# Keeping the weight's split operands for both token halves in the out-product of an MLP

## The chip, the cores and the metric

The kernel is one program on one core of a Trainium2 chip. The metric is the device time of one launch in microseconds (us): the median of several runs, each of them one execution. One more execution is recorded by the hardware profiler, and all rows shown here come from such a record. Engines are called as in the profile: PE is the matmul engine, PEld its weight load, DVE the vector engine, ACT the scalar engine, POOL the GpSimd engine, SP the queue that issues DMAs. Each engine takes its instructions in a fixed order, written when the program is built.

## The reference, cut to what matters

One layer of an encoder: an attention group beside a recurrent group, a cross-attention, then an MLP, for 2048 tokens of width 1024 in float32.

```python
D_MODEL, SEQ, D_FF = 1024, 2048, 4096
...
        hid = jnp.square(jax.nn.relu(rmsnorm(h, norm_mlp_g[l]) @ w_mlp_in[l]))
        h = h + hid @ w_mlp_out[l]
    return rmsnorm(h, norm_final_g).astype(x.dtype)
```

The change is in the second product, `hid @ w_mlp_out`, 4096 to 1024 wide. Everything before it is as it was.

## The kernel before

**Precision.** A float32 operand is split in two: a head h, an ACT copy into the type that PE reads (fp32r), and a remainder l, the operand less its head, by a subtraction on DVE or POOL. A product is then three matmuls, `mm3`: ah·bh, ah·bl, al·bh (lines 119 to 121).

**Fast products.** Both MLP products cut their operands in 2 x 2 blocks and use seven products of sums of blocks instead of eight (Winograd's form of Strassen's scheme). The in-product (`InPair`, 32 pairs) writes its result to DRAM as `hid_d`. The out-product runs in 16 passes: part q (0 to 7) takes 512 of the 4096 rows, and B (0 or 1) is the half of the tokens; pass n is q = n // 2, B = n % 2. In this document odd passes are those with B = 1. Operand A comes from the weight `w_m2` (four blocks of 128 x 1024, two of row halves by two of column halves) and depends on q alone; operand B comes from `hid_d` and depends on q and on the half. Pass 15 is plain: four operands, no sums.

**A part's work.** `Part.load` issues four DMAs of 512 KB (line 1269). `Part.sum_steps` makes the sums (an addition in line 1282, all others in `minus`, line 1257): of A all four on POOL, 1024 wide, of B two on DVE and two on POOL. `Part.split(n)` splits operand n (ACT in line 1304, remainder in line 1305): of A in two halves of 512, the remainders of operands 2 and 5 on DVE and of the other five on POOL; of B in one piece of 1024, remainder on DVE. Loads and sums of A are made once for each q, when B is 0. Its splits are made in every pass, for both halves of the tokens anew: seven operands, 14 ACT copies, 10 POOL and 4 DVE subtractions.

**Places.** On-chip memory is full, so tiles take over the places of tiles that are done. A `Ring` hands out a list of named places in turn. `A_RINGS` has five places for raw blocks, three for sums, eight for heads, eight for remainders; `B_RINGS` has five, three, four, four. A new tile waits for the last reader of the one whose place it takes, whichever engine that is.

**A pass.** Seven slots s, one product each: four 128-wide pieces d, by two, by `mm3`, so 24 matmuls of 128 x 512. A product adds into four PSUM banks (`SLOTS`, `BANKS`: names m, a, b in the profile), and after each piece DVE adds the bank into an accumulator in on-chip memory (line 1459, the evictions; accumulators are named t3l to t6h and wr). The next product that uses the same bank waits for that eviction. Slot 2 issues the next pass's loads, slot 4 its sums, slots 0 to 4 the splits of operands 2 to 6, slots 5 and 6 the next pass's operands 0 and 1. A planner then orders each engine's instructions by that priority and by when it expects operands and places to be there, so splits run ahead of products. The last pass is split in token ranges of 512, 256 and 256 and is followed by a final normalisation (`RowSum`, lines 137 to 164, and `finish`, lines 1419 to 1423).

Of the kernel before, what the change touches and what calls it, by code (L numbers as in the profile page):

```python
# [10 lines left out]
F32, F32R, F16, BF, I32 = DT.float32, DT.float32r, DT.float16, DT.bfloat16, DT.int32  # L11
AF = mybir.ActivationFunctionType
ALU = mybir.AluOpType
# [26 lines left out]
def hybrid_block(ctx: ExitStack, tc: tile.TileContext, prm, x, xT, mem, memT, pos, masks, w_in, gate_w,  # L40
                 w_out, w_cq, w_ck, w_cv, w_co, w_m1, w_m2, out):
    nc = tc.nc
    act, dve, pool, pe = nc.scalar, nc.vector, nc.gpsimd, nc.tensor
    dma = nc.sync.dma_start
    dma_r = nc.gpsimd.dma_start
    P = 128

    def f32(a):
        return a.bitcast(F32)
# [22 lines left out]
    hid_d = [[dt_(f"hid_d{i}_{p}", [2, 2, P, 512]) for p in range(16)] for i in range(2)]  # L72
# [50 lines left out]
    class RowSum:  # L123


        def __init__(self, pl, bufs=1, n=512, late=False, eng=pool, rings={}):
            self.pl, self.i, self.n, self.late, self.eng, self.rings = pl, 0, n, late, eng, rings
            self.ss = self.tile("ss", bufs)

        def tile(self, name, bufs):  # L130
            if name in self.rings:
                return self.rings[name]()[:, 0:self.n]
            return self.pl.tile([P, 512], F32, tag=name, name=name, bufs=bufs)[:, 0:self.n]
# [72 lines left out]
    with ExitStack() as s12:  # L206
# [400 lines left out]
        with sb("xr") as xr_pool:  # L607
            with sb("p1") as p1:
                W, steps = unit_w(w_in[0], True)
# [27 lines left out]
    with ExitStack() as s3:  # L637
# [321 lines left out]
        with sb("aw") as aw:  # L959
            half_out(aw, W)  # L960
            for k in range(8):
                t = aw.tile([P, 512], F32, tag="raw4", name="raw4", bufs=2)
# [6 lines left out]
    with ExitStack() as s6:  # L969
# [9 lines left out]
        for kk in range(4):  # L979
            for n in range(2):  # L980
                t = wp.tile([P, 512], F32, tag="ht", name="raw4", bufs=3)
# [149 lines left out]
        class InPair:  # L1131
# [5 lines left out]
            def load(self):  # L1137
                self.r = []
                for f in range(2):
                    t = wr_.tile([P, 8 * P])  # L1140
                    dma(t.rearrange("p (k n) -> p k n", n=P), w_m1[2 * self.p + f])
                    self.r.append(t)
# [9 lines left out]
            def split(self, n):  # L1152
                h, l = wh_.tile([P, 512], F32R), wl_.tile([P, 512], F32R)
                act.activation(h, self.a[n], AF.Copy)  # L1154
                last[n % 2] = (pool if n % 2 else dve).tensor_tensor(l, self.a[n], f32(h), op=ALU.subtract).ins  # L1155
                self.w[n] = h, l
# [99 lines left out]
    def minus(eng, o, x, y):  # L1256
        eng.tensor_tensor(o, x, y, op=ALU.subtract)  # L1257

    class Part:


        def __init__(self, rings, blocks, plain, eng, sum_eng):
            self.rings, self.blocks, self.plain, self.eng, self.sum_eng = rings, blocks, plain, eng, sum_eng
            self.s, self.b = {}, {}

        def load(self):
            for k, src in self.blocks:
                t = self.b[k] = self.rings["r"].tile([P, 2, 512])
                dma(t, src)

        def sums(self):
            for _ in self.sum_steps():
                pass

        def sum_steps(self):
            b, e = self.b, self.sum_eng
            if self.plain:
                self.ops = [b[0, 0], b[0, 1], b[1, 0], b[1, 1]]
                return
            x1, x2, x4 = (self.rings["s"].tile([P, 2, 512]) for _ in range(3))  # L1280
            if self.rings is A_RINGS:
                e[0].tensor_tensor(x1, b[1, 0], b[1, 1], op=ALU.add)
                yield
                minus(e[1], x2, x1, b[0, 0])
                yield
                minus(e[2], b[1, 0], b[0, 0], b[1, 0])
                yield
                minus(e[3], x4, b[0, 1], x2)
                self.ops = [b[0, 0], x2, x1, x4, b[1, 0], b[1, 1], b[0, 1]]
            else:  # L1290
                minus(e[0], x1, b[0, 1], b[0, 0])
                minus(e[1], x2, b[1, 1], x1)
                minus(e[2], b[0, 1], b[1, 1], b[0, 1])
                minus(e[3], x4, b[1, 0], x2)
                self.ops = [b[0, 0], x2, x1, b[1, 1], b[0, 1], x4, b[1, 0]]

        def split(self, n):
            t, w = self.ops[n], self.rings["w"]
            h, l = [], []
            for k in range(0, 2, w):  # L1300
                h.append(self.rings["h"].tile([P, 512 * w], F32R))
                l.append(self.rings["l"].tile([P, 512 * w], F32R))
                tk = t[:, k:k + w, :].rearrange("p k n -> p (k n)")
                act.activation(h[-1], tk, AF.Copy)  # L1304
                self.eng[n].tensor_tensor(l[-1], tk, f32(h[-1]), op=ALU.subtract)  # L1305
            cut = lambda x_: [x_[k // w][:, 512 * (k % w):512 * (k % w) + 512] for k in range(2)]
            self.s[n] = cut(h), cut(l)

    A_ENG = [pool, pool, dve, pool, pool, dve, pool]
    B_ENG = [dve] * 7  # L1310
    tt = [(jp, f"t{n}{z}{h}") for n in range(7) for z in "hl" for h in range(2)]
    rw = [(ip, f"raw{k}{h}") for k in ("00", "01", "11", "10", "t") for h in range(2)]
    c2 = [(jp, f"c{i}") for i in (2, 3, 4, 5, 6, 0, 1)]
    w2 = [(ip, f"w{k}{i}") for k in "hl" for i in range(3)]
    s2 = [(ip, f"ws{i}") for i in range(3)]
    A_RINGS = {"r": Ring(*rw[:5]), "s": Ring(*rw[5:8]), "h": Ring(*s2[:2], *c2[:2], *c2[3:7]),
               "l": Ring(s2[2], c2[2], *w2), "w": 1}
    B_RINGS = {"r": Ring(*rw[8:], *tt[:3]), "s": Ring(*tt[3:6]), "h": Ring(*tt[6:14:2]), "l": Ring(*tt[7:14:2]), "w": 2}
    acc_at = Ring(*tt[14:], (ip, "wr0"), (ip, "wr1"))

    def a_part(q, plain):

        blocks = []
        for i, k in ((0, 0), (1, 0), (1, 1), (0, 1)):
            r = 512 * q + 256 * k
            blocks.append(((i, k), w_m2[r:r + 256, 512 * i:512 * i + 512].rearrange("(t p) d -> p t d", p=P)))
        return Part(A_RINGS, blocks, plain, A_ENG, [pool] * 4)

    def b_part(q, B, plain):

        blocks = [((k, th), hid_d[B][2 * q + k][:, th].rearrange("f p n -> p f n"))
                  for k, th in ((0, 0), (0, 1), (1, 1), (1, 0))]
        return Part(B_RINGS, blocks, plain, B_ENG, [dve, dve, pool, pool])

    passes = []
    for q in range(8):
        a = a_part(q, False)
        for B in range(2):
            passes.append((q, B, a, b_part(q, B, q == 7 and B == 1)))

    last_a = a_part(7, True)
    passes[-1] = (7, 1, last_a, passes[-1][3])
    rings = {"ss": lambda: A_RINGS["s"].tile([P, 2, 512])[:, 0, :], "sq": lambda: B_RINGS["s"].tile([P, 2, 512])[:, 0, :],
             "dg": lambda: B_RINGS["s"].tile([P, 2, 512])[:, 0, :]}

    def begin(n, what):

        q, B, a, b = passes[n]
        if what == "load":
            if a.plain:  # L1350
                a.b.update(passes[n - 1][2].b)
                a.blocks = a.blocks[1:2]
            if B == 0 or a.plain:
                a.load()
            b.load()
        elif what == "sums":
            if B == 0 or a.plain:
                a.sums()
            b.sums()
        else:  # L1360
            a.split(what)
            b.split(what)

    T = {}
# [6 lines left out]
    steps = t_raws(1)  # L1371
    nT = {}
    for i, pr in enumerate(ins):
        if i == 16:
            T = nT
        for n in range(7):
            if n == 2 and 0 < i < 31:
                ins[i + 1].load()
            if n == 4 and i < 31:
                ins[i + 1].sums()  # L1380
            if n < 5:
                pr.split(n + 2)
            elif i < 31:
                ins[i + 1].split(n - 5)
            pr.product(n, T[n])
            if 9 <= i < 15:
                ahead(1)
            if i == 0 and n == 2:
                rb2.append(rows())
                before.ss.columns()  # L1390
                before.ss.rows(rb2[3])
            if i == 15 and n > 0:
                t_part(nT, n - 1)
            if i == 16 and n == 0:
                t_part(nT, 6)
            if i == 20 and n == 0:
                first_a.load()
                first_sums = first_a.sum_steps()
            if i in (21, 22, 23, 24, 25) and n == 3:
                with tc.issue_after(last[1]):  # L1400
                    next(first_sums, None)
            if i == 31:
                if n == 1:
                    first_b.load()
                if n == 4:
                    first_a.split(0)
                    first_a.split(1)
                if n == 5:
                    first_b.sums()
                    first_b.split(0)  # L1410
                    first_b.split(1)
# [159 lines left out]
```

## Time and profile before

| what | value |
|---|---|
| median of 3 runs | 2863.25 us (2860.2 to 2868.93) |
| profiled execution, its own time | 2856.53 us |
| its span, first to last instruction | 2854.7 us |
| mean granted clock of PE | 0.947 |
| in-product, splits of its weights to last eviction | 1449 to 2168 us of the span |
| out-product, passes 0 to 14 | 2167 to 2781 us |
| last pass and final normalisation | 2781 to 2855 us |
| ACT copies of A, passes 1 to 13 | 182 x 0.633 us |
| A remainders, passes 1 to 13 | 130 on POOL, 52 on DVE |

A row of a group reads: line, engine, operation, out<-in, shape, number of instructions | busy time, mean ns of one | idle time of the engine before them and what ended it. A row of waits reads: who waited <- for whom: us in total, times, longest. A row of a timeline reads: start, duration, engine, line, operation, tiles; x2 means two merged, and a bracket is idle time before it. Tiles are named by their place, so one name serves many contents: raw is an A block or sum, c, ws, wh and wl hold A heads and remainders, rawt and t0 B blocks and sums, t1 to t3 B's heads and remainders.

### The profile page before, as it was taken

What the parts mean: (1) busy time and instruction counts of PE and PEld (TensorE: products, weight loads), DVE (VectorE), ACT (ScalarE), POOL (GpSimd) and SP (SyncE); (2) the same over time, 40 slices, a digit from 0 to 9 for tenths busy, and PEclk for the clock granted to TensorE, in tenths of its full rate; (3) what the DMA queues carried; (4) which work ended last, traced back from release to release, by engine and by line L of the source; (5) the groups of instructions that cost most, each with busy time, mean ns of one, the idle gap of its engine ahead of it and who ended that gap; (6) DMA issues with size and microseconds to landing.
All of it is one profiled execution on the core that took longest, in us unless ns stands there. A gap on an engine that the chain in (4) does not pass through costs nothing. (4 is left out here: it accounts for less than half of the span.)

```text
span 2854.7 us, 39920 instructions
## 1 busy us (share of the span) xinstructions
PE 2541.4 (89%) x14104; PEld 2139.9 (75%) x14104; DVE 2013.0 (71%) x3257; ACT 1278.4 (45%) x2359; POOL 1351.6 (47%) x916
## 2 busy tenths in 40 slices
PE   8899785884887797999996999899998999999997
PEld 6778674773887786777875888788886777777876
DVE  7547676774888678446578554755548999999997
ACT  6438545452765566435333333433333333333452
POOL 3222121222776573542145555646655767666662
PEclk9999897986998898999998999999999999999998
DMA  6443334337786784653253333343335222222213
GB/s 212 145 129 98 117 108 144 102 106 184 202 234 170 185 209 114 217 168 101 89 173 112 114 111 111 111 144 112 109 109 203 74 82 81 82 67 89 82 45 118
DMA packets 258044, 368.43 MB, mean 129 GB/s; under 512 B 85682, under 2 KB 132018, under 8 KB 254772
## 3 DMA queue, kind: packets, MB, share of 16 engines
q1 hardware_dynamic: 253556, 338.62, 37.6%
q0 software_dynamic: 4288, 27.27, 3.9%
q8 instruction: 111, 1.82, 0.3%
q14 instruction: 89, 0.73, 0.1%
HBM read 251.19 MB, written 114.63 MB: 128 GB/s over the span
## 5 line engine op out<-in xcount | busy, mean ns | idle before, releaser
L1304 ACT ACTIVATE c<-raw 128x512 fp32r<-128x512 f32 x162 | 102.1, 632 | 273.0 <-PE m L120 140.8
L1155 POOL TENSOR_TENSOR wl<-wr,wh 128x512 fp32r<-128x512 f32 x96 | 145.5, 1516 | 145.7 <-ACT wh L1154 145.7
L1154 ACT ACTIVATE wh<-wr 128x512 fp32r<-128x512 f32 x128 | 80.9, 632 | 287.2 <-PE m L120 151.6
L757 ACT ACTIVATE sm<-sm,obp 128x256 f32<-128x256 f32 (+1 forms) x384 | 161.0, 469 | 59.6 <-DVE obp L754 52.8
L1155 DVE TENSOR_TENSOR wl<-ws,wh 128x512 fp32r<-128x512 f32 x96 | 81.0, 843 | 127.0 <-ACT wh L1154 127.0
L754 DVE CUSTOM_DVE_ANT_0 sm<-a,msk 128x256 f32<-128x256 f32 (+1 forms) x384 | 129.7, 372 | 38.7 <-PE a L751 36.5
L226 POOL TENSOR_TENSOR wl<-wraw,wh 128x512 fp32r<-128x512 f32 x48 | 71.3, 1487 | 166.9 <-ACT wh L225 160.2
L1176 DVE TENSOR_TENSOR c<-m,c 128x512 f32<-128x512 f32 x64 | 44.1, 690 | 138.4 <-PE m L121 136.4
L119 PE MATMUL m<-xh,wh 128*128 128x512 f32 x328 | 131.6, 401 | 8.0 <-ACT xh L320 8.0
L766 PE MATMUL b<-prt,sm 128*128 128x128 f32 x640 | 109.3, 286 | 29.2 <-DVE pl L770 13.7
L769 ACT ACTIVATE ph<-b 128x512 f16<-128x512 f32 (+1 forms) x192 | 100.1, 523 | 69.6 <-PE b L766 68.9
L1305 POOL TENSOR_TENSOR wh<-raw,c 128x512 fp32r<-128x512 f32 x58 | 94.7, 1650 | 76.6 <-ACT c L1304 71.5
L120 PE MATMUL m<-xl,wh 128*128 128x512 f32 x328 | 130.1, 397 | 0.0
L770 DVE SCALAR_TENSOR_TENSOR pl<-b,ph 128x512 f16<-128x512 f32 (+1 forms) x192 | 114.7, 598 | 21.4 <-ACT ph L769 19.0
L121 PE MATMUL m<-xh,wl 128*128 128x512 f32 x328 | 129.7, 396 | 0.0
L696 POOL TENSOR_SCALAR kc<-kh 128x1024 fp32r<-128x1024 f32 x32 | 66.0, 2062 | 121.7 <-PE a L751 97.5
L1177 DVE SCALAR_TENSOR_TENSOR c<-c 128x512 f32<-128x512 f32 x96 | 114.1, 1189 | 1.0
L121 PE MATMUL m<-t3h,wl 128*128 128x512 f32 x276 | 108.4, 393 | 2.0 <-POOL wl L1155 2.0
L1154 ACT ACTIVATE wh<-ws 128x512 fp32r<-128x512 f32 x96 | 60.4, 629 | 108.0 <-PE m L120 107.2
L766 PEld LDWEIGHTS b<-prt,sm 128*128 128x128 f32 x640 | 76.6, 146 | 34.8 <-issue 14.9
L1305 POOL TENSOR_TENSOR wl<-raw,c 128x512 fp32r<-128x512 f32 x58 | 93.3, 1625 | 19.8 <-ACT c L1304 19.8
L1033 POOL TENSOR_SCALAR pm<-pm,dn 128x256 f32<-128x256 f32 x64 | 36.6, 590 | 127.6 <-DVE dn L1031 112.4
(573 smaller groups left out, 9787.4 us busy)
## 6 DMA issues: line engine op xcount, KB each, us to landing
wr<-in_w_m SPq DMA_DIRECT2D x64, 512.0 KB
hid_d<-c SPq DMA_DIRECT2D x128, 256.0 KB
wraw<-in_w_in SPq DMA_DIRECT2D x80, 256.0 KB
raw<-in_w_m SPq DMA_DIRECT2D x33, 512.0 KB
rawt<-hid_d SPq DMA_DIRECT2D x26, 512.0 KB
t0h<-hid_d SPq DMA_DIRECT2D x26, 512.0 KB
o_d<-obp SPq DMA_DIRECT2D x16, 528.0 KB
obr<-o_d SPq DMA_DIRECT2D x16, 528.0 KB
```

The lines of the kernel that those rows point to most:

```text
L119: pe.matmul(o, ah, bh, start=start, stop=False, **kw)
L120: pe.matmul(o, ah, bl, start=False, stop=False, **kw)
L121: pe.matmul(o, al, bh, start=False, stop=stop, **kw)
L754: dve.tensor_tensor_reduce(out=sm, in0=sps[:, 256 * z + o0:256 * z + o0 + kw], in1=msk[:, m:m + kw], op0=ALU.add, op1=ALU.min, scale=1.0, ...
L757: exps.append(act.activation(sm, sm, AF.Exp, scale=-1.0, bias=self.obp[:, oc, 65:66]))
L766: pe.transpose(pt[:, c0:c0 + 128], self.sm[:, z, 128 * g:128 * g + 128], idt)
L770: dve.scalar_tensor_tensor(self.pl[:, :w], pt[:, :w], 1024.0, self.ph[:, :w], op0=ALU.mult, op1=ALU.subtract)
L1154: act.activation(h, self.a[n], AF.Copy)
L1155: last[n % 2] = (pool if n % 2 else dve).tensor_tensor(l, self.a[n], f32(h), op=ALU.subtract).ins
L1177: dve.scalar_tensor_tensor(z, z if n < 6 else o, 0.0, z, op0=ALU.max, op1=ALU.mult)
L1304: act.activation(h[-1], tk, AF.Copy)
L1305: self.eng[n].tensor_tensor(l[-1], tk, f32(h[-1]), op=ALU.subtract)
```

## The change

A's split operands are made when B is 0 and kept for B = 1. There is not room for 14 remainders beside 14 heads, raw blocks and sums, so remainders go to nine places shared with the raw blocks and sums: the remainder of an operand takes the place of the operand split before it, or of a free place. The table `free` says which place of part q becomes which of part q + 1. Sixteen places serve as one ring for heads. The fourth sum (x4) is taken out of the sums and made just before operand 1 is split. In the last pass three of the four A operands are the ones kept, and only block (1, 0), which a sum had overwritten, is loaded and split again. The two kinds of part get classes of their own; what `BPart` issues is what `Part` issued for B.

```diff
+    class APart:
+        L_AT = {(0, 0): "a", 2: (0, 0), 1: 2, 4: 1, (1, 0): 4, (1, 1): (1, 0), (0, 1): (1, 1)}
+        def tile(self, k, d=F32):
+            pl, tag = self.at[k]
+            return pl.tile([P, 2, 512], d, tag=tag, name=tag)
...
+        def sum_steps(self):
+            b = self.b
+            x1, x2 = b[1], b[2] = self.tile(1), self.tile(2)
+            pool.tensor_tensor(x1, b[1, 0], b[1, 1], op=ALU.add)
+            yield
+            minus(pool, x2, x1, b[0, 0])
+            yield
+            minus(pool, b[1, 0], b[0, 0], b[1, 0])
+            yield
+            b[4] = self.tile(4)
+            minus(pool, b[4], b[0, 1], x2)
+
+        def split(self, n, key=None):
+            key = A_OPS[n] if key is None else key
+            t = self.b[key]
+            lt = self.tile(self.L_AT[key], F32R)
             h, l = [], []
+            for k in range(2):
+                h.append(h_a.tile([P, 512], F32R))
+                l.append(lt[:, k, :])
+                act.activation(h[-1], t[:, k, :], AF.Copy)
+                A_ENG[n].tensor_tensor(l[-1], t[:, k, :], f32(h[-1]), op=ALU.subtract)
+            self.s[n] = h, l
+    A_OPS = [(0, 0), 2, 1, 4, (1, 0), (1, 1), (0, 1)]
     A_ENG = [pool, pool, dve, pool, pool, dve, pool]
...
-    A_RINGS = {"r": Ring(*rw[:5]), "s": Ring(*rw[5:8]), "h": Ring(*s2[:2], *c2[:2], *c2[3:7]),
-               "l": Ring(s2[2], c2[2], *w2), "w": 1}
+    h_a = Ring(*s2[:2], *c2[:2], *c2[3:7], s2[2], c2[2], *w2)
...
+    order = [(0, 0), (1, 0), (1, 1), (0, 1), 1, 2, 4, "a", "b"]
+    free = ["b", (0, 1), "a", (0, 0), 2, 1, 4, (1, 0), (1, 1)]
+    at = dict(zip(order, [*rw[:8], (ip, "wr2")]))
     for q in range(8):
+        if q > 0:
+            at = {k: at[f] for k, f in zip(order, free)}
+        a = APart(q, at)
...
-    last_a = a_part(7, True)
+    last_a = APart(7, {(1, 0): at["b"], 4: at[4]})
+    ss_at = Ring((ip, "ss"), at[0, 1])
...
         elif what == "sums":
-            if B == 0 or a.plain:
-                a.sums()
+            if new:
+                steps = a.sum_steps()
+                for _ in range(3):
+                    next(steps)
+                a.rest = steps
             b.sums()
+        elif a is last_a:
+            if what == 2:
+                a.split(2, (1, 0))
+            else:
+                a.s[what] = passes[n - 1][2].s[(0, 6, 2, 5)[what]]
+            b.split(what)
         else:
-            a.split(what)
+            if new:
+                if what == 1:
+                    next(a.rest, None)
+                a.split(what)
             b.split(what)
```

`new` is true where B is 0. The ss tile of the final normalisation, which lay in the ring of sums, gets two places of its own (`ss_at`). The numbers of operands in the text are those of `A_OPS`: operand 0 is block (0, 0), 1 is x2, 2 is x1, 3 is x4, 4 the difference made in place of (1, 0), 5 block (1, 1), 6 block (0, 1).

More of the change, by code (lines that the diff above doesn't have):

```diff
@@ L1257, in minus, with __init__ @@
         eng.tensor_tensor(o, x, y, op=ALU.subtract)
-    class Part:
-        def __init__(self, rings, blocks, plain, eng, sum_eng):
-            self.rings, self.blocks, self.plain, self.eng, self.sum_eng = rings, blocks, plain, eng, sum_eng
+    class BPart:
+        def __init__(self, q, B, plain):
+            self.q, self.B, self.plain = q, B, plain
             self.s, self.b = {}, {}
         def load(self):
-            for k, src in self.blocks:
-                t = self.b[k] = self.rings["r"].tile([P, 2, 512])
-                dma(t, src)
+            for k, th in ((0, 0), (0, 1), (1, 1), (1, 0)):
+                t = self.b[k, th] = B_RINGS["r"].tile([P, 2, 512])
+                dma(t, hid_d[self.B][2 * self.q + k][:, th].rearrange("f p n -> p f n"))
         def sums(self):
[L1272 to L1276, printed above, removed]
+            b = self.b
             if self.plain:
@@ L1279, in sum_steps @@
                 return
[L1280 to L1295, printed above, removed]
@@ L1297, in split @@
-        def split(self, n):
-            t, w = self.ops[n], self.rings["w"]
-            h, l = [], []
[L1300 to L1307, printed above, removed]
+            x1, x2, x4 = (B_RINGS["s"].tile([P, 2, 512]) for _ in range(3))
@@ new lines, in sums @@
+            minus(dve, x1, b[0, 1], b[0, 0])
+            minus(dve, x2, b[1, 1], x1)
+            minus(pool, b[0, 1], b[1, 1], b[0, 1])
+            minus(pool, x4, b[1, 0], x2)
+            self.ops = [b[0, 0], x2, x1, b[1, 1], b[0, 1], x4, b[1, 0]]
+        def split(self, n):
+            t = self.ops[n].rearrange("p k n -> p (k n)")
+            h, l = (B_RINGS[z].tile([P, 1024], F32R) for z in "hl")
+            act.activation(h, t, AF.Copy)
+            dve.tensor_tensor(l, t, f32(h), op=ALU.subtract)
+            self.s[n] = [[x_[:, 512 * k:512 * k + 512] for k in range(2)] for x_ in (h, l)]
@@ new lines, in hybrid_block, with __init__, load @@
+    class APart:
+        L_AT = {(0, 0): "a", 2: (0, 0), 1: 2, 4: 1, (1, 0): 4, (1, 1): (1, 0), (0, 1): (1, 1)}
+        def __init__(self, q, at):
+            self.q, self.at, self.b, self.s = q, at, {}, {}
+        def tile(self, k, d=F32):
+            pl, tag = self.at[k]
+            return pl.tile([P, 2, 512], d, tag=tag, name=tag)
+        def load(self, keys=((0, 0), (1, 0), (1, 1), (0, 1))):
+            for i, k in keys:
+                r = 512 * self.q + 256 * k
+                self.b[i, k] = self.tile((i, k))
+                dma(self.b[i, k], w_m2[r:r + 256, 512 * i:512 * i + 512].rearrange("(t p) d -> p t d", p=P))
+        def sum_steps(self):
+            b = self.b
+            x1, x2 = b[1], b[2] = self.tile(1), self.tile(2)
[11 more added lines that the diff above has]
+            lt = self.tile(self.L_AT[key], F32R)
+            h, l = [], []
+            for k in range(2):
[4 more added lines that the diff above has]
+            self.s[n] = h, l
@@ L1309, in hybrid_block @@
+    A_OPS = [(0, 0), 2, 1, 4, (1, 0), (1, 1), (0, 1)]
     A_ENG = [pool, pool, dve, pool, pool, dve, pool]
-    B_ENG = [dve] * 7
     tt = [(jp, f"t{n}{z}{h}") for n in range(7) for z in "hl" for h in range(2)]
@@ L1315, in hybrid_block @@
     s2 = [(ip, f"ws{i}") for i in range(3)]
-    A_RINGS = {"r": Ring(*rw[:5]), "s": Ring(*rw[5:8]), "h": Ring(*s2[:2], *c2[:2], *c2[3:7]),
-               "l": Ring(s2[2], c2[2], *w2), "w": 1}
-    B_RINGS = {"r": Ring(*rw[8:], *tt[:3]), "s": Ring(*tt[3:6]), "h": Ring(*tt[6:14:2]), "l": Ring(*tt[7:14:2]), "w": 2}
+    h_a = Ring(*s2[:2], *c2[:2], *c2[3:7], s2[2], c2[2], *w2)
+    B_RINGS = {"r": Ring(*rw[8:], *tt[:3]), "s": Ring(*tt[3:6]), "h": Ring(*tt[6:14:2]), "l": Ring(*tt[7:14:2])}
     acc_at = Ring(*tt[14:], (ip, "wr0"), (ip, "wr1"))
[L1321 to L1333, printed above, removed]
+    order = [(0, 0), (1, 0), (1, 1), (0, 1), 1, 2, 4, "a", "b"]
+    free = ["b", (0, 1), "a", (0, 0), 2, 1, 4, (1, 0), (1, 1)]
+    at = dict(zip(order, [*rw[:8], (ip, "wr2")]))
     passes = []
     for q in range(8):
-        a = a_part(q, False)
+        if q > 0:
+            at = {k: at[f] for k, f in zip(order, free)}
+        a = APart(q, at)
         for B in range(2):
-            passes.append((q, B, a, b_part(q, B, q == 7 and B == 1)))
-    last_a = a_part(7, True)
+            passes.append((q, B, a, BPart(q, B, q == 7 and B == 1)))
+    last_a = APart(7, {(1, 0): at["b"], 4: at[4]})
     passes[-1] = (7, 1, last_a, passes[-1][3])
-    rings = {"ss": lambda: A_RINGS["s"].tile([P, 2, 512])[:, 0, :], "sq": lambda: B_RINGS["s"].tile([P, 2, 512])[:, 0, :],
+    ss_at = Ring((ip, "ss"), at[0, 1])
+    rings = {"ss": lambda: ss_at.tile([P, 512]), "sq": lambda: B_RINGS["s"].tile([P, 2, 512])[:, 0, :],
              "dg": lambda: B_RINGS["s"].tile([P, 2, 512])[:, 0, :]}
@@ L1348, in begin @@
         q, B, a, b = passes[n]
+        new = B == 0
         if what == "load":
-            if a.plain:
-                a.b.update(passes[n - 1][2].b)
-                a.blocks = a.blocks[1:2]
-            if B == 0 or a.plain:
+            if a is last_a:
+                a.load([(1, 0)])
+            elif new:
                 a.load()
@@ L1356, in begin @@
         elif what == "sums":
-            if B == 0 or a.plain:
-                a.sums()
-            b.sums()
-        else:
-            a.split(what)
+            if new:
[3 more added lines that the diff above has]
+                a.rest = steps
+            b.sums()
+        elif a is last_a:
[4 more added lines that the diff above has]
+            b.split(what)
+        else:
+            if new:
+                if what == 1:
+                    next(a.rest, None)
+                a.split(what)
             b.split(what)
@@ L1405, in hybrid_block @@
                 if n == 4:
+                    next(first_sums, None)
                     first_a.split(0)
```

## The prediction

> **What bounds the kernel now.** I read the page's header and busy shares first, then stretches of 67 us (busy time of each engine, in brackets the instructions, then granted clock, DMA share, GB/s), then single passes of the out-product.
>
> ```profile
> span 2854.7 us, 39920 instructions
> PE 2541.4 (89%) x14104; PEld 2139.9 (75%) x14104; DVE 2013.0 (71%) x3257; ACT 1278.4 (45%) x2359; POOL 1351.6 (47%) x916
> ```
> ```profile
> 1975.00:2042.00 67.00, 67.00 (x297) 55.38 (x296) 32.66 (x37) 21.84 (x39) 40.94 (x26) 1.00 0.32 111
> 2377.00:2444.00 67.00, 63.60 (x278) 51.36 (x277) 63.89 (x67) 24.38 (x33) 49.48 (x25) 1.00 0.24 79
> ```
> ```profile
> 2295.40:2338.80 43.40, 40.16 (x175) 32.28 (x174) 40.95 (x43) 16.00 (x22) 33.76 (x18) 1.00 0.24 85
> 2338.80:2376.20 37.40, 37.24 (x165) 30.51 (x164) 35.14 (x42) 15.07 (x21) 20.39 (x13) 1.00 0.23 71
> 2376.20:2419.60 43.40, 40.16 (x175) 32.30 (x174) 40.98 (x42) 15.96 (x22) 33.76 (x18) 1.00 0.25 85
> sum 527.00, PE 503.35 PEld 408.21 DVE 497.47 ACT 202.04 POOL 358.80; mean PE 38.72 PEld 31.40 DVE 38.27 ACT 15.54 POOL 27.60
> ```
>
> The in-product (1975) starts a matmul every 67.00/296 = 0.2264 us and PE never stops. The out-product (2377) fits only 278 into the same time, and there DVE is busy 63.9 of 67. Cut at the last eviction of each pass, passes alternate: B = 1 takes 43.4 us, B = 0 takes 37.4, a pair 80.8. A pass issues 7 x 24 = 168 matmuls, so a pair needs 2 x 168 x 0.2264 = 76.1. The sum row covers passes 1 to 13: 527.0 us against 13 x 38.03 = 494.4, so **32.6 us are lost in seven B = 1 and six B = 0 passes**. Granted clock is 1.00 throughout. Who PE waited for there (in all us, times, longest; m and a are banks, t6l, wr and t5h accumulators):
>
> ```profile
> PE m L119 <- DVE wr L1459: 11.6, 7, 1.7
> PE m L119 <- DVE t6l L1459: 6.4, 7, 1.0
> PE a L119 <- DVE t6l L1459: 4.7, 7, 0.7
> PE m L119 <- DVE t5h L1459: 0.9, 6, 0.2
> ```
>
> Three waits in each of the seven odd (B = 1) passes, one short one in each of six even ones, all for DVE's evictions (L1459). The rest of the 32.6 is refilling after each wait. Why evictions are late shows in the chain of waits through odd pass 5 and in the timeline (start, us, engine):
>
> ```profile
> 2385.93 0.69 DVE ws L1305
> 2387.22 1.69 DVE c L1305
> 2390.39 1.20 DVE t1l L1305
> 2393.07 0.68 DVE t6l L1459
> 2393.74 2.72 DVE t1h L1257
> 2396.47 0.61 DVE wr L1459
> 2397.12 0.50 PE m L119
> ```
> ```profile
> 2387.14 2.65 DVE L1305 TENSOR_TENSOR c<-raw,ws 128x512 fp32r<-128x512 f32 x1
> 2390.32 2.83 DVE L1305 TENSOR_TENSOR t1l<-t1h,t1l 128x1024 fp32r<-128x1024 f32 x1
> 2402.11 3.39 DVE L1305 TENSOR_TENSOR t2l<-t0l,t2l 128x1024 fp32r<-128x1024 f32 x1
> 2407.82 1.21 DVE L1305 TENSOR_TENSOR t3h<-t1h,t3h 128x1024 fp32r<-128x1024 f32 x1
> ...
> 2386.85 2.39 POOL L1282 TENSOR_TENSOR raw<-raw,raw 128x1024 f32<-128x1024 f32 x1 [3.76 <-DVE ws L1305]
> 2389.32 6.06 POOL L1257 TENSOR_TENSOR raw<-raw,raw 128x1024 f32<-128x1024 f32 x2
> 2395.35 3.36 POOL L1257 TENSOR_TENSOR rawt<-rawt,rawt 128x1024 f32<-128x1024 f32 x1
> 2404.38 5.81 POOL L1305 TENSOR_TENSOR wh<-raw,c 128x512 fp32r<-128x512 f32 x3
> 2410.15 4.24 POOL L1305 TENSOR_TENSOR wl<-raw,c 128x512 fp32r<-128x512 f32 x3
> ```
>
> Two things delay DVE: an A remainder in its queue (ws and c, operand 5 of pass 5, 0.69 + 2.65 us), and its own SBUF subtractions running 2.65 to 3.39 us while POOL streams sums (2386.85 to 2404) instead of 0.69 and 1.21. DVE's queue is in order and PE reuses a bank one product later (5.4 us, less the 1.4 of its own matmuls), so an eviction over about 4 us late stops PE.
>
> [...] Evictions, whose one input is in PSUM, never stretch, and subtractions from SBUF do:
>
> ```profile
> L1459 DVE TENSOR_TENSOR t6l<-a,t6l 128x512 f32<-128x512 f32 x28 | 17.8, 675 | 0.0
> 2349.78 3.02 DVE L1305 TENSOR_TENSOR t2h<-t1h,t2h 128x1024 fp32r<-128x1024 f32 x1
> 2349.33 2.40 POOL L1257 TENSOR_TENSOR rawt<-t0h,rawt 128x1024 f32<-128x1024 f32 x1 [4.79 <-DVE wh L1305]
> 2214.50:2741.50 527.00, 240.19 (x143) 208.14 (x131) 1.00 0.23 79
> ```
>
> POOL's sum ended at 2351.73, and 3.02 is 1.95 of waiting for that plus 1.1 of work. The last row (line 1305 alone, DVE then POOL, same thirteen passes): 143 DVE remainders took 240.2 us; 91 B ones at 1.21 and 52 A ones at 0.69 would take 146, so 94 us, 0.66 each, was waiting. [...]
>
> **The change part by part.**
>
> *Removed in the odd passes 1 to 13.* Seven operands, two halves each: 14 ACT copies, 10 POOL and 4 DVE remainders per pass, 7 times. ACT is worth nothing (16 us busy in 43.4; PE sets its pace). POOL: 10 x 1.59 (208.14/131) = 15.9 us of 54.1 a pair (33.76 + 20.39). DVE: 4 x 0.69 = 2.8 undisturbed. Waiting falls with POOL's share, from 358.8/527 = 68% to (54.1 - 15.9)/76 = 50%: 26 SBUF operations a pair (14 B remainders, 4 B sums, 8 A remainders) at 0.66 become 22 at 0.49, 17.2 to 10.8 us. DVE gains 2.8 + 6.4 = 9.2 us a pair and needs about 4.6. It would be busy some 67 of 76.1 us, 88%, where the even pass is now at 35.14/37.40 = 94% and loses only the 0.2-us wait.
>
> *Moved.* Remainders now lie on raw tiles and sums, so the next part must wait for products of the odd pass. Counted from that pass's first matmul (product k ends at 5.44 x (k+1)): x1 goes where remainder 2 lay (16.3 us), x2 where remainder 3 lay (21.8), x4 where 4 lay (27.2), remainder 0 where 5 lay (32.6). Before, the A sums started at 10 to 11 us (2386.85 against 2376.2). POOL behind 16.3: A sums 4 x 2.4, B sums 2 x 2.4, remainders 0 and 1, 4 x 1.3: 19.6 us undisturbed, up to about 27 at the durations of the crowded rows. Remainder 0 is wanted at 38.06 + 0.45: two halves at 1.3 to 1.65 end at 35.2 to 35.9, and only what POOL is then in the middle of (at most 3.4) can make it late, by 0.8. I take nothing, bounds 0 and 0.8 a pair. Queued behind it on POOL are remainder 1, due 5.4 later, and any sum left over; PE alone waits for remainder 0.
>
> *Further remainders of the next part* (2 on DVE, 3 and 4 on POOL) now overwrite the place of the operand before, one after another, where today they run some three products ahead. Each link costs 0.7 to 3 us, against 5.44 of product: hidden, but if POOL is late, DVE's remainder 2 blocks the evictions behind it; bound 0 to 1 us a pair.
>
> *Loads.* As many A loads as before; (1,1) and (0,1) wait for products 0 and 1 (5.4 and 10.9 us) before their sums are due at 16.3 and 27.2. SP issues in order, so B's loads behind them shift by up to the same, against a B lead of near three products (t2l of pass 6 is made at 2402, before that pass starts near 2419). Nothing; bound 1 us a pair if that lead is used up.
>
> *x4 after remainder 0 in program order*, h tiles in one ring of 16 with 14 alive, ss in its own places: two free places cover operand 0, the others are freed one product at a time. Nothing, between -0.3 and +0.5 a pair, inside the moved terms.
>
> *Last pass.* Eight copies and eight remainders become two and two, the two left being DVE's.
>
> ```profile
> 2780.47 1.63 POOL L1305 TENSOR_TENSOR ws<-raw,ws 128x512 fp32r<-128x512 f32 x1 [1.04 <-ACT ws L1304]
> 2782.05 1.75 POOL L1305 TENSOR_TENSOR c<-raw,ws 128x512 fp32r<-128x512 f32 x1
> 2782.57 1.78 DVE L1305 TENSOR_TENSOR wl<-raw,c 128x512 fp32r<-128x512 f32 x1
> 2785.61 1.12 PE L163 MATMUL b<-t1h,all 128*128 128x512 f32 x2 [1.27 <-DVE t1h L160]
> ```
>
> Without the two POOL ones, wl takes 0.69, and PE's 1.27 us wait for the DVE queue behind it shrinks by about 1.1: -1.4 with the copies gone, bounds -3 and 0.
>
> *First pass.* Its A remainders no longer need tiles of the in-product, so the order may shift around this wait:
>
> ```profile
> 2199.75 0.77 PE L119 MATMUL a<-t2h,c 128*128 128x512 f32 x1 [3.37 <-DVE t4l L1459]
> 2200.74 0.63 PE L121 MATMUL a<-t2h,wh 128*128 128x512 f32 x1
> 2201.16 0.63 PE L119 MATMUL a<-t2h,c 128*128 128x512 f32 x1
> ...
> 2205.43 0.58 PE L120 MATMUL b<-t2h,c 128*128 128x512 f32 x1
> ```
>
> After it matmuls start every 0.42 us (2200.74 to 2201.16) until 2205.43, six us at little more than half pace. Zero, bounds -7 (it goes) and +7 (another like it).
>
> **The sum.** I leave 0.8 us in each odd pass (the even pass's small wait and one more, for the POOL stream after 16.3) and 0.4 in each even one: 7 x 0.8 + 6 x 0.4 = 8.0 of 32.6 stay, -24.6. With the last pass -26.0. The profiled execution took 2856.53 us, 6.7 below the median of 2863.25; it becomes 2830.5, the median 2837. The waits repeat to a tenth pass by pass, so the gain should stand in every execution. A run can tell about 0.3% (8.6 us) from no change.
>
> **Rivals.**
> 1. *Crowding moves along.* From 16.3 us POOL streams without a break. In four products (21.8 us) DVE then has 16 evictions at 0.61 (wr in the chain) = 9.8, and 4 B remainders and 2 B sums at 1.21 = 7.3; if each of the six meets half of a 2.4-us sum, 7.2 more: 24.3, 2.5 us short. Kept per pair, 7 x 2.5 = 17 stays beside the even passes' 2.4, gain 13 + 1: **2849**. For it: DVE at 2.65 to 3.39 whenever POOL streams. Against: POOL now pauses for products, and the A remainder is gone from that stretch.
> 2. *All of it goes*, and the first pass's wait too: -32.6 - 3 - 7: **2821**. For: the in-product with POOL at 41 of 67 never stops. Against: even passes with less POOL still wait.
> 3. *Late remainder, slower.* If two 1024-wide POOL operations stand before remainder 0 when product 5 ends, it comes 2 x 3.3 + 3.3 after 32.6, at 42.5: PE idles 4.0 us at each of seven boundaries. That equals what is removed; the point where it decides is two such sums. After 3.37 us idle the rows above show six us at 0.42 a matmul, so about 3 more us follow: 7 x (4.0 + 3.0) - 24.6 = +24: **2887**. For: POOL's order is fixed ahead. Against: all sums but x4 are ready by 21.8. [...]
> 4. *No change*: splitting vanishes but the serial chain of remainders costs what it saves, 4 us a pair: **2861**. Against: 5.44 us of product cover each link.
>
> **How the numbers follow.** Forecast 0.57 (own range 2828 to 2846), rival 1 0.16, rival 2 0.11, rival 4 0.09, rival 3 0.07. Faster 0.57 + 0.16 + 0.11 = 0.84, same 0.09, slower 0.07. Taking in rivals 1 and 2 and part of the bounds: 2820 to 2857.
>
> **What would show it.** Right: odd passes near 38.5 us, pairs near 77.3, the three waits for t6l and wr gone or under 0.4, 28 fewer DVE and 76 fewer POOL operations at the split line, DVE near 88%, A sums starting after product 2 of odd passes. Wrong: PE waiting for a POOL remainder at the start of even passes (rival 3), DVE subtractions over 2.4 us late in odd passes with PE waiting (rival 1), or evictions behind a DVE remainder that waits for POOL (rival 4).

## The result, and the profile after

The changed kernel is slower: 2880.07 us (2874.54 to 2883.49, six runs) against 2861.72 (2854.23 to 2868.93, six runs), a ratio of 1.0057 with a 95% interval of 1.0042 to 1.0073. Its profiled execution took 2877.05 us. The page begins:

```profile
span 2875.3 us, 39380 instructions
PE 2553.4 (89%) x14104; PEld 2146.7 (75%) x14104; DVE 1938.3 (67%) x3229; ACT 1217.1 (42%) x2255; POOL 1234.1 (43%) x840
```

The counts are those forecast: DVE 3257 to 3229, POOL 916 to 840, and ACT 104 fewer. DVE went from 2013.0 to 1938.3 us busy, POOL from 1351.6 to 1234.1. PE runs the same 14104 matmuls, and yet the span grew by 20.6 us. In these two executions 6.3 us of it lie ahead of the out-product's first eviction (2170.14, now 2176.39); 2.4 of these are a longer wait of PE for the in-product's last remainder from POOL (2.1 us, now 4.5), and the rest is not explained. Offsets of up to 14 us at this point stand between the profiled executions of the kernels below too. In the last pass 2.4 us were won (113.2 us from the end of pass 13 to the end of the span, now 110.8). The rest is in the passes. By single passes after the change (time, busy time of each engine, clock, DMA share, GB/s; passes 4 to 6, then the sum of passes 1 to 13):

```profile
2350.20:2389.60 39.40, 37.08 (x158) 29.07 (x157) 33.07 (x41) 8.19 (x9) 16.73 (x8) 1.00 0.21 67
2389.60:2431.90 42.30, 40.91 (x181) 33.53 (x181) 31.58 (x40) 14.42 (x20) 23.11 (x11) 1.00 0.28 87
2431.90:2473.40 41.50, 37.00 (x158) 29.07 (x157) 35.54 (x40) 8.22 (x9) 14.69 (x8) 1.00 0.19 64
sum 543.70, PE 512.08 PEld 411.99 DVE 427.98 ACT 150.12 POOL 259.76; mean PE 39.39 PEld 31.69 DVE 32.92 ACT 11.55 POOL 19.98
```

Odd passes became 1.1 us shorter, where 4.9 were expected (43.4 to 42.3), and even ones, which were to stay near their 37.4, longer: 39.2 to 39.5 us, in pass 6 41.5 and in pass 10 43.3. DVE is busy 31.6 of 42.3 us in an odd pass: it is no longer short, and PE still waits. The waits of PE in passes 1 to 13:

```profile
PE m L119 <- DVE t5h L1490: 7.9, 6, 2.9
PE m L119 <- DVE t5l L1490: 5.8, 1, 5.8
PE m L119 <- DVE t3l L1490: 4.7, 10, 0.5
PE a L119 <- ACT c L1331: 4.4, 3, 1.5
PE m L119 <- DVE t4l L1490: 3.5, 5, 0.7
```

The three waits of before, for t6l and wr in odd passes, are gone but for 0.3 us twice. New are: one of about 1.5 us at a late place in each odd pass (the row that names ACT c, with single rows for wh, ws and wl); several short ones in each even pass (t3l, t4l, t5h); 2.7 and 2.9 us in passes 6 and 10 alone (the longest of t5h); and 5.8 us once, at the end of pass 1. How the odd one comes about stands in the timelines of ACT, POOL, DVE and PE in pass 5, which prepares part 3. (Lines after the change: A's copies 1331, its remainders 1332; B's 1287 and 1288; sums 1257 and 1314; evictions 1490, in some kernels below 1491.)

```profile
2410.85 1.16 ACT L1331 ACTIVATE wl<-raw 128x512 fp32r<-128x512 f32 x2 [4.53 <-POOL raw L1314]
2413.34 1.15 ACT L1331 ACTIVATE c<-wr 128x512 fp32r<-128x512 f32 x2 [1.33 <-POOL wr L1257]
2414.40 1.04 ACT L1287 ACTIVATE t2l<-t0l 128x1024 fp32r<-128x1024 f32 x1
...
2407.42 3.40 POOL L1314 TENSOR_TENSOR raw<-wr,raw 128x1024 f32<-128x1024 f32 x1
2410.90 2.41 POOL L1257 TENSOR_TENSOR wr<-raw,wr 128x1024 f32<-128x1024 f32 x1
...
2410.70 0.69 DVE L1490 TENSOR_TENSOR t6h<-m,t6h 128x512 f32<-128x512 f32 x1 [0.34 <-PE m L121]
2415.47 1.27 DVE L1288 TENSOR_TENSOR t2l<-t0l,t2l 128x1024 fp32r<-128x1024 f32 x1 [4.08 <-ACT t2l L1287]
2416.67 1.27 DVE L1490 TENSOR_TENSOR t6l<-a,t6l 128x512 f32<-128x512 f32 x2
...
2417.49 0.47 PE L119 MATMUL a<-t1l,c 128*128 128x512 f32 x1 [1.39 <-ACT c L1331]
```

ACT's first two instructions here are A's copies of operands 2 and 4; both wait for POOL's sums, x1 (2407.42) and the difference of operand 4 (2410.90), which now start only after product 2. Behind them in ACT's queue stands B's copy t2l, 24.8 us after the pass began at 2389.6. DVE's remainder of t2l waits 4.08 us for that copy, the eviction of bank a (2416.67) stands behind the remainder, and PE stands still until 2417.49. (The row names ACT because an A copy ended in the same instant; no matmul of this pass reads it. What PE needs there is the bank.) So DVE's time is not short any more; it is spent waiting for ACT, which is busy 14.4 of 42.3 us.

### The profile page after: what moved, and what is told of

It is laid out like the page before. It is cut to its first block, busy times and chain, and to the rows that moved or that the text cites. A ratio compares the mean times of both kernels' runs of the same rounds, so it can differ in the third digit from the quotient of the medians.

```text
span 2875.3 us, 39380 instructions
## 1 busy us (share of the span) xinstructions
PE 2553.4 (89%) x14104; PEld 2146.7 (75%) x14104; DVE 1938.3 (67%) x3229; ACT 1217.1 (42%) x2255; POOL 1234.1 (43%) x840
## 5 line engine op out<-in xcount | busy, mean ns | idle before, releaser
L121 PE MATMUL m<-xh,wl 128*128 128x512 f32 x328 | 130.7, 398 | 0.0
L750 PE MATMUL a<-kc,qc 128*128 128x256 f32 x256 | 79.5, 329 | 14.8 <-POOL qc L696 14.7
L225 ACT ACTIVATE wh<-wraw 128x512 fp32r<-128x512 f32 x96 | 58.4, 624 | 74.8 <-DMA wraw<-in_w_in 39.1
L1149 POOL TENSOR_TENSOR ws<-wr 128x512 f32<-128x512 f32 x32 | 42.9, 1339 | 105.4 <-DMA wr<-in_w_m 100.5
L120 PE MATMUL r<-rl,woh 128*128 128x256 f32 x256 | 76.8, 300 | 12.1 <-DVE rl L670 12.1
```

The costliest lines, as they stand in the source:

```text
L120: pe.matmul(o, ah, bl, start=False, stop=False, **kw)
L121: pe.matmul(o, al, bh, start=False, stop=stop, **kw)
```

## Experiments

Ratios are to the kernel before, measured again beside each group of runs (its median there was 2861 to 2864 us).

**The sums may start sooner.** `free_places`, one line in `compute` ahead of the products:

```diff
                 (ah, al), (bh, bl) = a.s[s], b.s[s]
+                if B:
+                    al = a.s[6][1]
```

> The changed kernel, but in odd passes 1 to 13 every product reads the remainder of operand 6 in place of its own (so that part of the computation is changed); instructions are as many as in the changed kernel. The places of remainders 0 to 5 come free after the even pass, so the next part's sums and remainders wait for no product of the odd pass. Theory 'places' (the waits for places that products of the odd pass still hold cost everything): the forecast of the change comes true, odd and even passes lose under 1.5 us each, 2830 to 2845 us, about 35 to 45 below the changed kernel. Rival 'order' (what costs is how the engines' queues were rearranged, whatever the places): still above 2865.

Measured 2852.05 us, ratio 0.996 (0.9944 to 0.9976). Passes 3 to 12 took 385.4 us, where the changed kernel has 414.3 and the kernel before 403.8: a pair of 77.1. The median lies above the expected range all the same: in the profiled execution the out-product began 5.6 us later than the changed kernel's, and passes 0 and 1 took 50.8 and 44.8 us (in the changed kernel 44.4 and 47.7); why stays open. The late release of places is necessary for the loss in steady passes.

**ACT's queue alone.** `act_order` leaves all places as they are and puts each A copy behind B's copy of the same number on ACT:

```diff
-            act.activation(h, t, AF.Copy)
+            self.copy = act.activation(h, t, AF.Copy).ins
...
+            b.split(what)
             if new:
                 if what == 1:
                     next(a.rest, None)
-                a.split(what)
-            b.split(what)
+                with tc.issue_after(b.copy):
+                    a.split(what)
```

> The changed kernel; on ACT each copy of A's operand is put behind the copy of B's operand of the same number. Theory 'ACT queue' (A's copies wait for A's late sums, B's copy stands behind them, DVE's B remainder behind that and the evictions behind it): the wait of 1.6 us in odd passes and the one of 6 us at the end of pass 1 go, 6 x 1.6 + 8 = 18 us, 2860 to 2865. Rival 'chain' (the losses come from remainders that wait for one another at the start of even passes): odd passes gain at most 1 us each and it stays above 2870.

Measured **2840.23 us, ratio 0.9921 (0.9896 to 0.9946)**. Passes 3 to 12 of before, of the changed kernel, of `free_places` and of `act_order` (time first, then busy time of PE, PEld, DVE, ACT and POOL):

```profile
2295.40:2699.20 403.80, 386.72 (x1682) 313.83 (x1681) 380.52 (x411) 155.14 (x211) 270.70 (x141) 1.00 0.23 79
```
```profile
2307.90:2722.20 414.30, 391.04 (x1681) 314.12 (x1680) 328.36 (x390) 113.03 (x141) 195.41 (x90) 1.00 0.24 77
```
```profile
2316.60:2702.00 385.40, 382.44 (x1682) 314.95 (x1681) 345.04 (x391) 114.74 (x141) 194.09 (x90) 1.00 0.27 82
```
```profile
2306.40:2692.60 386.20, 383.65 (x1682) 314.50 (x1682) 333.76 (x391) 110.83 (x141) 203.72 (x90) 1.00 0.27 82
```

Five pairs in 386.2 us are 77.24 each; the prediction said 77.3. The gain, 40 us, is over twice the 18 expected: the short waits of even passes went too (all waits of PE from 2300 to 2733 us are five, of 2.5 us together), which the theory did not have. The instructions on every engine are the changed kernel's; only the order in ACT's queue, and what the planner makes of it on the others, differs. So late sums do little harm by themselves; they do when A's copies wait for them ahead of B's.

**Both edits together.** `both` tells whether the places still cost anything.

> All of A's copies behind B's as in act_order, and besides the odd passes read the remainder of operand 6 in every product (their output is not the reference's), so that the other places come free after the even pass. If with the copies in order the waits for places cost nothing more (my theory): steady pairs within 0.4 us of act_order's 77.25, 2836 to 2844 us, 0.991 to 0.994 of before. If the places still cost (rival): what is left above 76.1 goes, 7 x 1.1 = 8 us less, 2832.

Measured 2839.79 us, 0.9916 (0.9887 to 0.9945), passes 3 to 12 in 387.1 us. No difference to `act_order`: the two edits remove the same loss from its two ends.

**Which copies.** `act_01` orders the copies of operands 0 and 1 alone, `act_26` those of 2 to 6 (a condition on `what` at `tc.issue_after`; B's split stays first in the program for all operands).

> act_order for operands 0 and 1 alone; copies of A's operands 2 to 6 go where the planner puts them. Theory 'two losses' (copies 0 and 1 that wait for late sums hold up B's copies in odd passes; copies 2 to 6 made all at once crowd the start of even passes): the odd passes' wait of 1.6 us goes, the even passes' 2.4 to 3.5 us stays, 2860 to 2868. Rival 'one loss' (it is only A's copies ahead of B's in ACT's queue at the end of the odd pass, and the even passes' waits follow from it): as act_order, 2838 to 2845.

> act_order for operands 2 to 6 alone. Theory 'two losses': the even passes' waits go, the odd passes' 1.6 us and the 6 us at the end of pass 1 stay, 2850 to 2858. Rival 'one loss': the same as the changed kernel within 5 us if the copies of operands 0 and 1 are what holds B's copies up; or as act_order, 2838 to 2845, if those of 2 and 3 are.

`act_01`: 2878.59 us, 1.0057 (1.0036 to 1.0078), as the changed kernel: neither these two nor B's split being first in the program gains anything. `act_26`: 2839.46 us, 0.9919 (0.9894 to 0.9943), as `act_order`. Then 2 to 6 in parts: 2 and 4, 4 alone, and 3, 5 and 6.

> The changed kernel, ACT copies of A's operands 2 and 4 alone (the two that wait for POOL's sums) placed behind B's copies of the same number; 3, 5 and 6 keep the planner's place. If those two hold up B's copy, DVE's remainder behind it and the evictions (my theory): odd passes lose 0 to 0.4 us, even ones 0.2 to 0.8, pairs near 77.5, 2839 to 2843 us, 0.992 to 0.993 of before. If what matters is that all copies are spread one to a product, so that remainders do not come in a bunch (rival): odd passes lose nothing but even ones still 2 to 3.5, 7 x 3 us worse than that, near 2860.

> The changed kernel, A's operand 4 alone copied behind B's copy of operand 4. Theory: A's copy of operand 2 still waits for x1 ahead of B's copy, but B's copy then starts about 2.4 us sooner (2413.34 to 2414.40 and the 1.33 us waited go), more than the 1.5 us that PE waits in odd passes: odd passes lose 0.5 or less. Remainder 4 of the chain comes later, so the bunch in even passes thins out: 1 to 2.5 of 3.6 us left. 2848 to 2862 us, 0.995 to 1.000 of before. Rival, operand 2 is what holds B up: nothing changes, 2875 to 2880.

> The changed kernel, A's operands 3, 5 and 6 copied behind B's copies, 2 and 4 left where the planner puts them: the complement of act_24. Theory: the odd passes' wait stays (1.5 to 1.7 us), the bunch of remainders in even passes thins (3.6 to about 2): 2865 to 2875 us, 1.001 to 1.005 of before. Rival, spreading all is what matters and 2 and 4 do not: 2840 to 2850.

`act_24` 2855.93 us, 0.9972 (0.9953 to 0.999); `act_4` 2853.88, 0.9968 (0.9952 to 0.9985); `act_356` 2853.34, 0.9964 (0.9947 to 0.998). Each part gives over half of the way to `act_26`. `act_4` came out as expected, `act_24` and `act_356` nearer the rival's numbers: my theory gave too much to operands 2 and 4. The waits of PE from 2300 to 2733 us (passes 3 to 12 and most of pass 13) show that these are two losses. In `act_24` none is left in odd passes, and the short ones of even passes stay:

```profile
PE m L119 <- DVE t4l L1491: 5.7, 5, 1.2
PE m L119 <- DVE t3l L1491: 4.4, 10, 0.5
```

In `act_356` the odd one stays, now put down to the eviction itself, and the even ones shrink:

```profile
PE a L119 <- DVE t6l L1491: 8.8, 6, 1.5
PE m L119 <- DVE t6h L1491: 2.2, 5, 0.4
PE m L119 <- DVE t4l L1491: 2.2, 5, 0.7
```

In `act_26` there is nearly nothing (passes 1 to 13; the row for L121 belongs to the boundary into pass 2 alone):

```profile
PE m L119 <- DVE t6h L1491: 3.5, 7, 0.7
PE m L121 <- POOL raw L1332: 2.3, 2, 2.0
```

Over passes 3 to 12 `act_26` takes 385.9 us, `act_24` 395.2, `act_356` 398.8. Of the 28.4 us that the changed kernel has more than `act_26`, 9.3 are thus the even passes' waits, 12.9 mainly the odd ones', and some 6 are the extra waits of passes 6 and 10, which either part removes (41.5 and 43.3 us against 39.4). Since `act_4` alone takes the odd wait to zero too (its rows are those of `act_24` within 0.3 us), it is the copy of operand 4 that makes B's eviction late enough; operand 2's wait is covered.

Why early copies of 3, 5 and 6 cost the even passes is shown less fully. DVE and POOL at the boundary into pass 6, in the changed kernel and then in `act_26`:

```profile
2429.37 0.69 DVE L1332 TENSOR_TENSOR raw<-raw,wl 128x512 fp32r<-128x512 f32 x1 [1.24 <-POOL raw L1332]
2431.18 0.68 DVE L1490 TENSOR_TENSOR t6h<-m,t6h 128x512 f32<-128x512 f32 x1
2431.78 2.00 DVE L1257 TENSOR_TENSOR t0l<-t0l,t0h 128x1024 f32<-128x1024 f32 x1
...
2434.31 1.70 DVE L1288 TENSOR_TENSOR t2h<-rawt,t2h 128x1024 fp32r<-128x1024 f32 x1
...
2431.41 3.51 POOL L1332 TENSOR_TENSOR raw<-raw,ws 128x512 fp32r<-128x512 f32 x2 [2.07 <-DVE raw L1332]
...
2440.47 3.51 POOL L1332 TENSOR_TENSOR raw<-raw,c 128x512 fp32r<-128x512 f32 x2 [2.07 <-DVE wr L1332]
```
```profile
2417.39 0.69 DVE L1332 TENSOR_TENSOR raw<-raw,wl 128x512 fp32r<-128x512 f32 x1 [2.60 <-POOL raw L1332]
2419.19 1.22 DVE L1257 TENSOR_TENSOR t0l<-t0l,t0h 128x1024 f32<-128x1024 f32 x1
2420.33 0.68 DVE L1491 TENSOR_TENSOR t6h<-m,t6h 128x512 f32<-128x512 f32 x1
2421.53 1.21 DVE L1288 TENSOR_TENSOR t2h<-rawt,t2h 128x1024 fp32r<-128x1024 f32 x1
...
2419.42 4.48 POOL L1332 TENSOR_TENSOR raw<-raw,ws 128x512 fp32r<-128x512 f32 x2 [2.07 <-DVE raw L1332]
...
2438.34 2.16 POOL L1332 TENSOR_TENSOR raw<-raw,c 128x512 fp32r<-128x512 f32 x1 [1.89 <-DVE wr L1332]
```

With all heads ready early, the chained remainders 3 to 6 run in one stretch: POOL starts operand 3 at 2431.41 and operand 6 at 2440.47, 9 us later. With the copies spread, the same two start at 2419.42 and 2438.34, 19 us apart. In the bunch DVE's sum t0l and subtraction t2h take 2.00 and 1.70 us instead of 1.22 and 1.21, and t0l stands behind the last eviction of the pass instead of ahead of it. The planner moved that sum by itself when the copies moved, so order and stretching aren't told apart here. DVE's wait for POOL's remainder does not by itself tell the two kernels apart: it is 1.24 us in the changed kernel and 2.60 in `act_26`, and all such waits for the place raw in passes 3 to 12 sum to 11.1 and 11.7 us.

**A's loads behind B's.** `load_order`, with `self.loaded` set at B's last load:

```diff
+            b.load()
+            with tc.issue_after(b.loaded):
                 if a is last_a:
                     a.load([(1, 0)])
                 elif new:
                     a.load()
-            b.load()
```

> The changed kernel; on the SP queue A's four loads for a pass are put behind B's four loads for the same pass. Theory 'SP queue' (a load of A that waits for a place holds up B's loads; DVE's B sum then waits 2.4 us for its data in passes 6 and 10 and evictions behind it): the waits of 2.9 and 3.1 us in passes 6 and 10 go, and what follows them at half pace, 8 to 9 us in all, 2870 to 2873. Rival: those waits are the two engines' sums excluding each other, and it stays within 4 us of the changed kernel.

Measured 2875.91 us, 1.0052 (1.0035 to 1.0069): no net gain that stands clear of noise. It does settle the longer waits of passes 6 and 10. In the changed kernel, SP, DVE and PE there:

```profile
2444.00 0.37 SPq L1309 DMA_DIRECT2D raw<-in_w_m  x1
2444.47 0.42 SPq L1270 DMA_DIRECT2D rawt<-hid_d  x1
2449.25 3.43 DVE L1257 TENSOR_TENSOR t1h<-rawt,t0l 128x1024 f32<-128x1024 f32 x1 [2.28 <-DMA rawt<-hid_d]
2453.33 0.50 PE L119 MATMUL m<-t2h,ws 128*128 128x512 f32 x1 [2.74 <-DVE t5h L1490]
```

An A load waits for a remainder's place (POOL's remainder of operand 6, 2440.47 above, ends at 2443.98, and the load goes out at 2444.00). B's load stands behind it in SP's queue, B's sum waits 2.28 us for the data and then takes 3.43 beside a sum on POOL (2449.22 to 2451.60), and the eviction behind it is late. With the loads exchanged that wait shrank to 0.2 us in both passes (each to 39.0 us), while the odd passes' grew from about 1.5 to about 2.1.

**All remainders on POOL.** `all_pool` takes DVE out of the chain: `A_ENG = [pool] * 7`.

> The changed kernel with all of A's remainders on POOL (operands 2 and 5 were on DVE). Theory 'chain' (DVE's A remainders wait for POOL's in the chain of places, and evictions stand behind them): the four short waits at the start of even passes, 2.4 us together, go in seven passes: 17 us, 2861 to 2865. Rival 'crowding' (those waits come from POOL and DVE excluding each other in that stretch): the same 28 operations take twice as long on POOL, and the time is 2875 to 2890.

Measured 2914.84 us, 1.0192 (1.0161 to 1.0223), far outside both expectations. PE's waits from 2300 to 2800 us, and SP and DVE in an even pass:

```profile
PE m L119 <- DVE t4l L1490: 48.1, 10, 9.3
```
```profile
2367.22 0.37 SPq L1309 DMA_DIRECT2D wr<-in_w_m  x1
2367.70 0.92 SPq L1270 DMA_DIRECT2D t0h<-hid_d  x2
2373.95 1.23 DVE L1257 TENSOR_TENSOR t1h<-t0h,t0l 128x1024 f32<-128x1024 f32 x1 [12.03 <-DMA t0h<-hid_d]
```

Each even pass has one wait of some 9 us (five of the ten in the row; the others are about 0.3). By these rows it is what `load_order` took out, larger: POOL's longer chain frees the places later, B's loads stand behind A's (POOL's last remainder ends at 2367.20, and A's load goes out at 2367.22), and DVE stands 12 us with evictions behind its sum. No run has both edits. The short waits for t3l, and those of up to 0.7 us for t4l, at the start of even passes are gone here, as theory 'chain' has it, but the later wait hides any gain, and DVE has 28 operations less as well. So what DVE's share in the chain costs is not settled.

**The late remainder at pass 2.** In `act_order` passes 0 to 2 still lose; `late1` adds that, for pass 2 alone, B's two POOL sums and x4 are issued behind remainder 0.

> act_order, and for pass 2 alone, on POOL, B's two sums and A's x4 behind A's remainder 0, which waits for product 5 of pass 1. In act_order POOL makes these three sums first there, and PE waits 2.2 and 1.6 us and runs some 6 us at half pace. Theory 'late remainder' (three sums stand before remainder 0 because the first sum started late in pass 1): 5 to 7 us less than act_order, 2833 to 2836. Rival (the sums are wanted as early, so the wait moves to operands 3 to 5 of pass 2): within 2 us of act_order.

Measured 2841.89 us, 0.993 (0.9906 to 0.9953): no gain. The 2.0-us wait for POOL's remainder is gone, and at 2261.82 PE waits 5.96 us for the eviction of t6h instead.

**The order without the change.** `before_act` is the kernel before with the order of `act_order`.

> The kernel before with act_order's edit: each copy of A's operand on ACT behind the copy of B's of the same number. Theory (ACT's order matters only where A's sums are late, as in the changed kernel; here DVE and POOL crowding each other is the bound): within 5 us of the kernel before. Rival 'order alone' (the edit would have gained the same without the change): 2835 to 2845.

Measured 2874.46 us, 1.0039 (1.0023 to 1.0055): some 10 us slower, outside the 5 expected, with one longer wait of PE in each odd pass in place of three (passes 1 to 13):

```profile
PE a L119 <- DVE t6l L1460: 23.8, 7, 3.7
```

So the order by itself is no gain. In steady passes it pays where the places come free late (414.3 to 386.2 us) and not where they come free early (`free_places` 385.4, `both` 387.1).

## Why the prediction was wrong

*What held.* The counts; the relief of DVE and POOL; the three odd-pass waits for late evictions gone; A sums behind product 2 (x1 at 2407.42, 17.8 us after the cut between the passes; 16.3 after the first matmul was forecast); the last pass, 2.4 us shorter where -1.4 stood, within its bounds. Waiting on DVE fell: in passes 1 to 13 the subtractions and sums of DVE (lines 1288, 1332, 1257: instructions, busy time) are

```profile
2220.80:2764.50 543.70, 149.65 (x92) 0.99 0.25 77
2220.80:2764.50 543.70, 17.87 (x26) 104.71 (x65) 0.99 0.25 77
2220.80:2764.50 543.70, 41.16 (x25) 132.59 (x47) 0.99 0.25 77
```

208.7 us for 143 operations; at 1.21 (117 of them) and 0.69 (26) they would take 159.5, so 0.34 us each is waiting, where 0.49 was forecast and 0.66 stood before. That it falls with POOL's busy share was my estimate, and no run shows it; what the traces show is the single operation's wait. Of the 233 subtractions and sums of 128x1024 that DVE made in passes 1 to 13 of the two kernels, 105 took 1.21 to 1.23 us. The other 128 (72 before, 56 after) took 1.27 to 3.43: each had started while a POOL instruction ran and ended 1.08 to 1.09 us after that one. None of the 364 evictions of 128x512 in either kernel took over 0.69 us, and 250 of them before and 180 after ran beside POOL.

*The step that failed: "ACT is worth nothing (16 us busy in 43.4; PE sets its pace)".* Busy time was the wrong reading. What matters of ACT is what stands at the head of its queue and what that waits for. The paragraph on moved steps put A's sums 5 to 6 us later, and I asked only who waits on POOL and PE for them, not who waits behind the copy that waits for them. None of the four rivals and none of the signs of being wrong looked at ACT. Price, odd and even passes together: 39.8 us, `act_order` against the changed kernel, of the 43 between the forecast and the result.

*"h tiles in one ring of 16 with 14 alive ... Nothing."* The eight places of before let A's heads in only a few products ahead, so a copy came to ACT about when its product was near. The ring of 16 takes seven operands at once, and nothing spreads the copies any longer. In pass 5 the trace has copies of operands 2 and 4 (2410.85 and 2413.34) ahead of B's. That the ring is the reason is argued from the code; a smaller ring was not tried. What runs show is that spreading the copies by hand suffices.

*"Further remainders ... hidden; bound 0 to 1 us a pair."* The even passes took some 2 us more than before (39.4 against 37.4), besides the load waits of passes 6 and 10. Rival 4 named the chain of remainders. Its sign, evictions behind a DVE remainder that waits for POOL, is there (2429.37 and the rows behind it), but `act_26` has a longer such wait and PE loses almost nothing. What part it has stays open.

*Loads, "Nothing; bound 1 us a pair".* About 3 us in two of seven pairs in the changed kernel, 9 in every pair in `all_pool`: the lead of B's loads is smaller than I read it from the one row of t2l.

*Rival 3, the late remainder,* came at one boundary, in `act_order`, `act_26` and `act_356` into pass 2 (2.0 us, the row for L121 above), not at seven. The first pass's wait of 3.37 us became two, of 2.9 and 1.1 us; pass 0 took 44.4 us before and after.

The sum itself, from DVE's shortage, was right once the new waits were gone, in a kernel that was not the one forecast: DVE is busy 66.8 us a pair, forecast 67; a pair takes 77.2, forecast 77.3; 2840, forecast 2837. That the pair agrees to 0.1 us is partly luck: the 0.8 and 0.4 us left in it were allowances, and by single passes it is 41.9 and 35.3 us where two passes of some 38.5 were forecast.

## What to carry to other kernels

An in-order engine that is idle more than half of the time can still set the pace, as ACT did here with 14.4 of 42.3 us busy: when a change makes an input later, look for every instruction that waits for it, and for what stands behind that instruction in its queue. A shortage of places also paces work; who adds places must say what paces it then. After a loss, the order of one queue is worth a trial before the idea is given up: here it turned 0.6% slower into 0.8% faster than the kernel before.

## What the runs showed of the hardware

Whether matmuls run at half pace after a wait of PE isn't set by the length of the wait alone. Where the kernel before starts one every 0.43 us (2200.3 to 2205.4) its granted clock is 0.50, and where it starts one every 0.23 us (2206 to 2210) it is 1.00. Two waits of the same length in one execution of `load_order` (its timeline):

```profile
2337.23 0.60 PE L119 MATMUL a<-t2l,ws 128*128 128x512 f32 x1 [1.98 <-ACT c L1331]
2337.63 0.63 PE L120 MATMUL a<-t2l,ws 128*128 128x512 f32 x1
...
2584.20 0.47 PE L119 MATMUL a<-t1l,c 128*128 128x512 f32 x1 [1.98 <-ACT ws L1331]
2584.51 0.39 PE L120 MATMUL a<-t1l,c 128*128 128x512 f32 x1
```

After the first 1.98 us the matmuls start 0.40 to 0.43 us apart (2337.23 to 2338.48), after the second 0.31 and then 0.23 us. In the changed kernel the 2.74 us (2453.33 above) were followed by starts 0.34, 0.24 and then 0.23 us apart at a granted clock of 1.00 (2453.4 to 2457), and the 2.90 us of pass 10, which end at 2618.78, by starts 0.42 to 0.44 us apart until 2622.21, at 0.53 (2618.8 to 2622.2). What decides between the two is not shown here.
